# Split weights at staggered places in SBUF and right-hand pools 192 bytes lower, in a two-layer decoder trunk

## The chip, the cores and the metric

The kernel runs on one core of one Trainium2 chip. The metric is device time in microseconds (us) of one execution. In traces and groups the engines are PE (TensorE, matmul), PEld (its weight load), DVE (VectorE), ACT (ScalarE), POOL (GpSimd) and SP (SyncE, which issues most transfers).

## The reference

Two pre-norm residual layers and a final norm, on one sequence of 1024 tokens, width 1024, in float32. Layer 0 mixes with eight retention heads and eight RWKV-7 heads that share one input and one output projection; layer 1 with sliding-window attention of 16 heads over 4 key/value heads. Each layer ends with a SwiGLU FFN of inner width 2816. Cut to what matters:

```python
for layer in range(2):
    h = rms_norm(x, norm1_g[layer])
    x = x + (retention_rwkv_mixer(h, ...) if layer == 0 else swa(h, ...))
    h = rms_norm(x, norm2_g[layer])
    x = x + (silu(h @ w_gate[layer]) * (h @ w_up[layer])) @ w_down[layer]
return rms_norm(x, final_g)
```

Nearly all of the arithmetic is in the projections and the FFN: float32 products of weights with activations.

## The kernel before

**Split products.** A float32 product is made from two halves in the reduced float32 type of PE (`F32R`). Each operand is split into a high part (a cast on ACT) and a low part (the operand minus the high part, a subtract on POOL, or on DVE where `self.lo` says so). `gemm` (L339 on) and `prod` (L1166 on) then issue three matmuls for each 128 x 128 block of weights: high by high, high by low, low by high (L345 to L347, L1169 to L1171; L239 where the mixer's planner issues them). Each of them loads 128 columns of weights, the stationary operand, and streams 512 columns of activations, the moving operand.

**Stages.** Tokens are taken in two halves of 512. Layer 0's mixer runs first, its order set by a planner (`Plan`) that keeps a running estimate of PE's time and picks chains and projection jobs by it. Then come the out projection of the first and of the second half, the FFN of layer 0 (gate and up in an early and a late part, then down), the attention of layer 1, its FFN and the final norm. The gate, up and down products are made by a seven-product scheme for 2 x 2 blocks (`early`, `late`, `form0`, `form1`); the late part streams combinations of activations that lie in the tiles `cb`, the early part streams the tiles `n8` (shown as `n`).

**Weights.** A raw block of 1024 columns is loaded to one of two places `wr` (L298). `wsplit` (L321 on) makes one or two split blocks of it, each 2 x 512 columns of 4 bytes, high part then low part. `wtile` (L312 on) gives the place for a split block: four rotating places `w` of 4096 bytes each in the left pool `pp`; in the late FFN the two `wr` places too; in the attention stage two places `wx` in the right-hand pool `at`; in a part of the down projection places `wd1` only. `wkept` (L305 on) takes the same four places for split blocks that are read back from DRAM.

**Where tiles lie.** Pools are stacks of SBUF: left ones grow upward from the bottom, right-hand ones downward from the top. `pp` is the lowest left pool and stays open; a tile `pad` of 120 columns is at the top of the right-hand stack. So the size of the `w` places shifts all that is allocated after them on the left (such as `n8` in `pp` and the later left pools), and the size of `pad` shifts every right-hand pool (such as `cb`, `at`, and `nB`, which holds an `n8` of layer 1). In bytes of a partition, before: `wr` at 2176 and 6272, `w` at 10368, 14464, 18560 and 22656, `n8` in `pp` from 27264, `pad` at 228864. Modulo 512: `w` and `wr` 128, `n8` on the left and `ha` 128, `n8` in `nB` 0, `cb` 0, `wx` 256, `wd1` 128.

**What sets the order.** The instructions of each engine are put in order when the kernel is built, by a scheduler with its own estimate of times; it works with tags and the number of buffers of each, not with addresses. On the chip each engine takes its instructions in that order and waits on semaphores.

Of the kernel before, what the change touches and what calls it, by code (L numbers as in the profile page):

```python
# [10 lines left out]
F32 = mybir.dt.float32  # L11
F32R = mybir.dt.float32r
# [4 lines left out]
P = 128  # L17
T = 1024
HT = 512
# [2 lines left out]
FT = 22  # L22
DGROUPS = [[(0, 4), (4, 8)], [(0, 4), (4, 8), (8, 11)]]
NP = FT // 2
CW = math.exp(-0.5)
NCH = 8
RMS_EPS = 1e-6
# [77 lines left out]
class Plan:  # L105
# [3 lines left out]
    def __init__(self, K):  # L109
        self.K, self.now, self.ev, self.banks = K, 0.0, {}, []  # L110
        self.gens, self.jobs, self.cur, self.twice = [], deque(), None, ()
# [93 lines left out]
class Kern:  # L205
    def __init__(self, ctx, tc, A, out):
        self.ctx, self.tc, self.nc, self.A, self.out = ctx, tc, tc.nc, A, out
        nc = self.nc
        self.pp = ctx.enter_context(tc.tile_pool(name="pp", bufs=1, side="left"))
        self.dr = ctx.enter_context(tc.tile_pool(name="dr", bufs=2, space=bass.MemoryType.DRAM))  # L210
        self.n = 0
        pad = ctx.enter_context(tc.tile_pool(name="pad", bufs=1, side="right"))
        pt = pad.tile([P, 120], F32, tag="pad", name="pad")
        nc.gpsimd.memset(pt, 0.0)
        nc.scalar.activation(pt[:, :16], pt[:, :16], AF.Copy)
        self.pv = self.t(self.pp, [P, NPV], "pv")
        nc.scalar.dma_start(self.pv, A["pvec"])
        self.cst = {}
        for nm in ("ones", "eps"):
            self.cst[nm] = self.const(self.pp, nm)  # L220
        self.h, self.plan = [None, None], None
        self.wx = None
        self.w6, self.nw, self.owed, self.lo = False, 0, [], self.nc.gpsimd
        self.hid = [self.dram(f"hid{i}", [FT, P, HT]) for i in range(4)]
        self.hc = [self.dram(f"hc{L}", [NP, 4, P, 2, HT]) for L in range(2)]
        self.bd = self.dram("bd", [KT, P, HT])
        self.u0d = self.dram("u0", [NP, 2, P, HT])
        self.wsp = self.dr.tile([30, 2, P, 2, HT], F32, tag="wsp", name="wsp", bufs=1)
        self.cats = [self.dram(f"cat{hf}", [KT, P, HT]) for hf in range(2)]
# [73 lines left out]
    def wkept(self, kept):  # L303

        res = []  # L305
        for i in range(2):
            w = self.t(self.pp, [P, 2, HT], "w", 4, F32R)
            self.nc.sync.dma_start(w.bitcast(F32), kept[i])
            res += [(w[:, 0, k * P : k * P + P], w[:, 1, k * P : k * P + P]) for k in range(4)]
        return res  # L310

    def wtile(self):  # L312

        pool, tag, n, only = self.wx or (None, "", 0, False)
        if only:
            return self.t(pool, [P, 2, HT], tag, n, F32R)
        i = self.nw = (self.nw + 1) % (6 if self.w6 else 4 + n)
        if i >= 4 and n:
            return self.t(pool, [P, 2, HT], tag, n, F32R)
        return self.t(self.pp, [P, 2, HT], *(("w", 4) if i < 4 else ("wr", 2)), F32R)  # L320

    def wsplit(self, raw, width=1024, keep=None):
        nc = self.nc
# [321 lines left out]
    def pair(self, u, hf, p):  # L645
# [38 lines left out]
        pw = self.t(mp, [P, HT], "rt", 6)  # L684
        S.activation(pw, cs, AF.Exp, scale=-CW)
        S.activation(cs, cs, AF.Exp, scale=CW)
        S.activation(s, s, AF.Exp, scale=-CW)
        PC = self.t(mp, [P, NCH], "PC", 4)
# [520 lines left out]
    def uses(self, L, p, sp, x=None):  # L1209
# [8 lines left out]
        def up(nm, c):  # L1218
            o = x[nm] if x else sg[nm]
            V.tensor_tensor(out=o, in0=sg[nm], in1=c, op=ALU.mult)  # L1220
            d = self.hid[2 * L + int(nm[1]) - 1][2 * p + int(nm[0]) - 1]
            if x and p == NP - 1:
                self.owed.append((d, o))
# [26 lines left out]
    def late_splits(self, L, wp):  # L1250

        def load(p):
            raws = [[self.rawtile(wp) for _ in range(2)] for _ in range(2)]
            for j in range(2):
                for i, nm in enumerate(("gate", "up")):
                    self.nc.sync.dma_start(raws[i][j], self.A[f"w_{nm}{L}"][2 * p + j])
            return raws

        nxt = load(0)
        for p in range(NP):  # L1260
            ws = [self.wsums(r, wp[0]) for r in nxt]
            if p == 0:
                yield
            if p + 1 < NP:
                nxt = load(p + 1)
# [25 lines left out]
    def form_down(self, L, p, x, ts):  # L1291
# [3 lines left out]
        def put(i, o, a, b):  # L1295
# [3 lines left out]
            d = (self.hc[L][p, i - 1], t.bitcast(F32))  # L1299
            if p == NP - 2 and i > 2:  # L1300
                self.owed.append(d)
# [188 lines left out]
    def attn(self, hf, nr, ap, n8):  # L1490
# [6 lines left out]
        def proj(ti, out, **kw):  # L1497
            w = self.wload(self.A["w_qkv"][ti])
            ps = self.pst("f", [P, HT])
            self.gemm(ps, w, nT)  # L1500
            V.tensor_tensor(out=out, in0=ps, in1=r, op=ALU.mult)
            S.activation(out, out, AF.Identity, **kw)
# [19 lines left out]
        for i, vc in enumerate(vcs):  # L1522
            pt = self.pst("m", [P, 4, P])
# [6 lines left out]
        for g in range(4):  # L1530
            for i in (2 * g, 2 * g + 1):
                proj(i, qt[i], scale=0.125, bias=b8[:, i : i + 1])
            for b in range(4):
                ti, rg = g // 2, g % 2
                k0 = 1 if (hf == 0 and b == 0) else 0
                kw = slice(P * k0, 256)
                nk = 256 - P * k0
                s = self.t(ap, [P, 4, 256], "s", 3)
                for e in range(2):
                    ps = self.pst("rc"[e], [P, 2, 256])  # L1540
                    a = slice(64 * e, 64 * e + 64)
                    src = (kc if e == rg else ks)[ti]
                    for i in range(2):
                        nc.tensor.matmul(
                            ps[:, i, kw], qt[2 * g + i][a, P * b : P * b + P], src[a, P * b + P * k0 : P * b + 256],
                            start=True, stop=True,
                        )
                    V.tensor_tensor(
                        out=s.rearrange("p (i e) k -> p e i k", e=2)[:, e, :, kw], in0=ps[:, :, kw],
                        in1=amask[:, kw].rearrange("p (o t) -> p o t", o=1).to_broadcast([P, 2, nk]), op=ALU.add,  # L1550
                    )
                st4 = self.t(ap, [P, 4, 4], "st4", 4)
                m, den, es = st4[:, 0, :], st4[:, 1, :], st4[:, 2, :]
                V.tensor_reduce(out=m, in_=s[:, :, kw], axis=AX.X, op=ALU.max)
                sk = sink[:, 4 * g : 4 * g + 4]
                V.tensor_tensor(out=m, in0=m, in1=sk, op=ALU.max)
                V.tensor_tensor(out=es, in0=sk, in1=m, op=ALU.subtract)
                V.tensor_scalar(out=m, in0=m, scalar1=-1.0, scalar2=None, op0=ALU.mult)
                S.activation(es, es, AF.Exp)
                for h in range(4):  # L1560
                    S.activation(
                        s[:, h, kw], s[:, h, kw], AF.Exp, bias=m[:, h : h + 1], accum_out=den[:, h : h + 1]
                    )
                V.tensor_tensor(out=den, in0=den, in1=es, op=ALU.add)
                V.reciprocal(out=den, in_=den)
                for h in range(4):
                    V.tensor_scalar(
                        out=s[:, h, kw], in0=s[:, h, kw], scalar1=den[:, h : h + 1], scalar2=None, op0=ALU.mult
                    )
                pT = self.t(ap, [P, 2, 4, P], "pT", 3)  # L1570
                for kb in range(k0, 2):
                    pt = self.pst("m", [P, 4, P])
                    for h in range(4):
                        nc.tensor.transpose(pt[:, h, :], s[:, h, P * kb : P * kb + P], ident)
                    if kb == 0:
                        S.copy(pT[:, kb], pt)
                    else:
                        V.tensor_copy(pT[:, kb], pt)
                po = self.pst("y", [P, 2, P])
                for e in range(2):  # L1580
                    a = slice(64 * e, 64 * e + 64)
                    pv4 = pT.rearrange("p k (i e) t -> p k e i t", e=2)
                    for kb in range(k0, 2):
                        nc.tensor.matmul(
                            po[a], vt[:, b + kb, 64 * g : 64 * g + 64], pv4[:, kb, e],
                            start=kb == k0, stop=kb == 1,
                        )
                tk = slice(P * b, P * b + P)
                hi, lo_ = n8[g][:, :, tk], n8[4 + g][:, :, tk]
                S.copy(hi, po)  # L1590
                V.tensor_tensor(out=lo_, in0=po, in1=hi.bitcast(F32), op=ALU.subtract)
# [234 lines left out]
```

## Time and profile before

| | us |
|---|---|
| median of 3 runs | 2416.72 |
| the runs | 2416.71, 2416.72, 2421.27 |
| span of the profiled execution | 2420.2 |
| PE busy in it | 2338.5 |
| DVE busy | 1635.1 |
| POOL busy | 1204.0 |
| ACT busy | 1035.8 |

All numbers from the trace belong to the one profiled execution. A row of groups gives line, engine, operation, output and inputs by the program's names without their numbers, partitions by columns, count, then the busy time of all in us and the mean of one in ns, then the idle time of the engine just ahead of them and what ended it. The ends of matmuls are modelled and overlap with the next start; their starts are recorded, and the timeline gives them in us from the start of the span.

### The profile page before, as it was taken

To read this page: it belongs to the slowest core of one execution; us is meant where nothing else is said; L and a number is where in the kernel's file an instruction comes from. 1 tells how busy PE (TensorE), PEld (TensorE's weight loads), DVE (VectorE), ACT (ScalarE), POOL (GpSimd) and SP (SyncE) were. 2 spreads that over 40 slices of the span, in tenths; PEclk is the share of its full clock that TensorE was granted. 3 is DMA by queue.
4 is the path that set the end of the run, shared out by engine and by line. 5 is a ranking of instruction groups with operands and counts; after the bars stand their busy time and mean duration, and the time that the engine had idled before them with its cause. 6 is when DMAs were issued, how large, how long until landed. Compare 5 with 4: busy or idle time off the path is not lost. (4 is left out here: it accounts for less than half of the span.)

```text
span 2420.2 us, 35718 instructions
## 1 busy us (share of the span) xinstructions
PE 2338.5 (97%) x13098; PEld 1838.3 (76%) x13098; DVE 1635.1 (68%) x2478; ACT 1035.8 (43%) x1914; POOL 1204.0 (50%) x975
## 2 busy tenths in 40 slices
PE   8999899989999999999999999999999999999997
PEld 6676677777777888887778877677678788887885
DVE  5766764776556457887675459558628787888776
ACT  5354543223555433333333545456635333333336
POOL 6555431221442057776577632342231677777665
PEclk9999999899999999999999999999999999999999
DMA  7564453434344645653564322142236466546652
GB/s 257 188 213 176 158 161 116 146 117 121 130 171 153 217 152 207 211 202 134 186 258 148 128 73 64 53 133 70 93 121 214 158 217 214 211 179 246 237 204 108
DMA packets 167742, 395.93 MB, mean 164 GB/s; under 512 B 42896, under 2 KB 45584, under 8 KB 167568
## 3 DMA queue, kind: packets, MB, share of 16 engines
q1 hardware_dynamic: 164448, 388.15, 47.2%
q10 hardware_dynamic: 2832, 4.45, 0.6%
q8 instruction: 104, 1.70, 0.3%
q0 software_dynamic: 288, 1.05, 0.1%
q14 instruction: 70, 0.57, 0.1%
HBM read 271.29 MB, written 116.92 MB: 160 GB/s over the span
## 5 line engine op out<-in xcount | busy, mean ns | idle before, releaser
L331 POOL TENSOR_TENSOR w<-wr,w 128x512 fp32r<-128x512 f32 x196 | 264.6, 1355 | 450.3 <-ACT w L330 391.5
L239 PE MATMUL ps_f<-n,w 128*128 128x512 f32 x1440 | 386.6, 417 | 13.5 <-ACT w L330 5.7
L239 PEld LDWEIGHTS ps_f<-n,w 128*128 128x128 f32 x1440 | 270.5, 193 | 97.3 <-issue 23.0
L330 ACT CAST w<-wr 128x512 fp32r<-128x512 f32 x244 | 148.0, 612 | 185.5 <-PE ps_f L347 77.5
L331 POOL TENSOR_TENSOR w<-wq,w 128x512 fp32r<-128x512 f32 x92 | 131.5, 1440 | 33.4 <-ACT w L330 28.8
L345 PE MATMUL ps_f<-n,w 128*128 128x512 f32 x356 | 142.2, 399 | 3.5 <-ACT n L351 2.6
L346 PE MATMUL ps_f<-n,w 128*128 128x512 f32 x356 | 142.9, 401 | 0.0
L347 PE MATMUL ps_f<-n,w 128*128 128x512 f32 x356 | 141.7, 398 | 0.0
L1176 DVE TENSOR_TENSOR nq<-ps_m,u 128x512 f32<-128x512 f32 x88 | 58.7, 684 | 108.8 <-PE ps_m L1171 108.5
L1169 PE MATMUL ps_f<-n,w 128*128 128x512 f32 x322 | 127.2, 396 | 4.1 <-DVE h L1369 1.8
L1170 PE MATMUL ps_f<-n,w 128*128 128x512 f32 x322 | 126.4, 392 | 0.0
L1171 PE MATMUL ps_f<-n,w 128*128 128x512 f32 x322 | 125.8, 391 | 0.0
L353 POOL TENSOR_TENSOR n<-nq,n 128x512 fp32r<-128x512 f32 x64 | 106.1, 1670 | 10.9 <-ACT n L351 10.9
L1171 PE MATMUL ps_m<-n,w 128*128 128x512 f32 x282 | 110.3, 391 | 0.0
L1170 PE MATMUL ps_m<-n,w 128*128 128x512 f32 x282 | 110.3, 391 | 0.0
L1169 PE MATMUL ps_m<-n,w 128*128 128x512 f32 x282 | 109.8, 390 | 0.0
L331 POOL TENSOR_TENSOR wx<-wr,wx 128x512 fp32r<-128x512 f32 (+1 forms) x38 | 49.3, 1299 | 105.0 <-ACT wx L330 105.0
L1169 PE MATMUL ps_m<-cb,w 128*128 128x512 f32 x240 | 94.8, 395 | 0.8 <-ACT w L330 0.8
L1171 PE MATMUL ps_m<-cb,w 128*128 128x512 f32 x240 | 94.8, 395 | 0.0
L1170 PE MATMUL ps_m<-cb,w 128*128 128x512 f32 x240 | 94.7, 395 | 0.0
L1343 POOL TENSOR_TENSOR w<-wd,w 128x512 fp32r<-128x512 f32 (+1 forms) x53 | 77.1, 1465 | 33.3 <-ACT w L1342 33.3
L345 PEld LDWEIGHTS ps_f<-n,w 128*128 128x128 f32 x356 | 67.4, 189 | 21.7 <-ACT n L351 3.0
(525 smaller groups left out, 6495.5 us busy)
## 6 DMA issues: line engine op xcount, KB each, us to landing
hc<-n SPq DMA_DIRECT2D x74, 512.0 KB, 2.7
wsp<-w SPq DMA_DIRECT2D x54, 512.0 KB, 3.4
w<-wsp SPq DMA_DIRECT2D x54, 512.0 KB, 3.6
wq<-in_w_gate SPq DMA_DIRECT2D x44, 512.0 KB, 3.9
u<-u SPq DMA_DIRECT2D x88, 256.0 KB, 2.9
n<-hc SPq DMA_DIRECT2D x43, 512.0 KB, 5.2
wr<-in_w_in SPq DMA_DIRECT2D x34, 512.0 KB, 4.8
hid<-n SPq DMA_DIRECT2D x66, 256.0 KB, 2.0
```

The source lines that it names most:

```text
L239: self.nc.tensor.matmul(out, lhsT, rhs, **kw)
L330: nc.scalar.copy(hi[:, :n], raw[:, c])
L331: self.lo.tensor_tensor(out=lo[:, :n], in0=raw[:, c], in1=hi.bitcast(F32)[:, :n], op=ALU.subtract)
L345: nc.tensor.matmul(ps, hi, rh, start=k == 0, stop=False)
L346: nc.tensor.matmul(ps, hi, rl, start=False, stop=False)
L347: nc.tensor.matmul(ps, lo, rh, start=False, stop=k == n - 1)
L353: e.tensor_tensor(out=lo, in0=src, in1=hi.bitcast(F32), op=ALU.subtract)
L1169: mm(ps, hi, xh, start=first and k == 0, stop=False, skip_group_check=True)
L1170: mm(ps, hi, xl, start=False, stop=False, skip_group_check=True)
L1171: mm(ps, lo, xh, start=False, stop=last and k == len(w) - 1, skip_group_check=True)
L1176: add = lambda o, x, y: V.tensor_tensor(out=o, in0=x, in1=y, op=ALU.add)
L1343: nc.gpsimd.tensor_tensor(out=lo, in0=v, in1=hi.bitcast(F32), op=ALU.subtract)
```

## The change

The four places for split weights, one tag with four buffers before, become four tags `w0` to `w3` with one buffer each, taken in turn by a new function `wplace`. Each place is longer by an unused piece: 16, 16, 8 and 8 columns of 4 bytes, that is 64, 64, 32 and 32 bytes. `pad` grows from 120 to 168 columns, 192 bytes. The small tile `st4` of the attention, four buffers of 64 bytes, becomes four of 128, of which the first 64 are used; this lowers what is allocated below it in `at` (such as `wx`) by 256 bytes more.

```diff
+WPAD = (16, 16, 8, 8)
...
-        pt = pad.tile([P, 120], F32, tag="pad", name="pad")
+        pt = pad.tile([P, 168], F32, tag="pad", name="pad")
...
+        self.iw = 3
...
-            w = self.t(self.pp, [P, 2, HT], "w", 4, F32R)
+            w = self.wplace()
...
-        return self.t(self.pp, [P, 2, HT], *(("w", 4) if i < 4 else ("wr", 2)), F32R)
+        return self.wplace() if i < 4 else self.t(self.pp, [P, 2, HT], "wr", 2, F32R)
+
+    def wplace(self):
+
+        self.n, self.iw = self.n + 1, (self.iw + 1) % 4
+        w = self.pp.tile([P, 2 * HT + WPAD[self.iw]], F32R, tag=f"w{self.iw}", name=f"w{self.iw}_{self.n}", bufs=1)
+        return w[:, : 2 * HT].rearrange("p (a b) -> p a b", b=HT)
...
-                st4 = self.t(ap, [P, 4, 4], "st4", 4)
+                st4 = self.t(ap, [P, 32], "st4", 4)[:, :16].rearrange("p (a b) -> p a b", b=4)
```

After: `wr` at 2176 and 6272 as before, `w0` to `w3` at 10368, 14528, 18688 and 22816, `n8` in `pp` from 27456, `pad` at 228672. Modulo 512: `wr` and `w0` 128, `w1` 192, `w2` 256, `w3` 288, every moving tile of a split product 320, `wx` and `wd1` 320.

Every engine but DVE has as many rows in its order as before (PE 8885, POOL 971); no instruction is added or removed. The scheduler moves a few blocks against each other. In the rows below, a name is followed by the numbers of its tiles, and lines of the changed kernel are larger by 8.

On PE, in the out projection of the second half of layer 0, two column blocks of weights follow each other, `ps_f_7034` and `ps_f_7068`. Before:

```order
L345 MATMUL ps_f_7034<-n_1002_6799,w_7031 128x512
L346 MATMUL ps_f_7034<-n_1006_6803,w_7031 128x512
L347 MATMUL ps_f_7034<-n_1002_6799,w_7031 128x512
L345 MATMUL ps_f_7034<-n_1002_6799,w_7031 128x512
L346 MATMUL ps_f_7034<-n_1006_6803,w_7031 128x512
L347 MATMUL ps_f_7034<-n_1002_6799,w_7031 128x512
```

After:

```order
L354 MATMUL ps_f_7034<-n_1006_6803,w_1057_7031 128x512
L353 MATMUL ps_f_7068<-n_1000_6797,w_1060_7062 128x512
L354 MATMUL ps_f_7068<-n_1004_6801,w_1060_7062 128x512
L355 MATMUL ps_f_7068<-n_1000_6797,w_1060_7062 128x512
L353 MATMUL ps_f_7068<-n_1000_6797,w_1060_7062 128x512
L354 MATMUL ps_f_7068<-n_1004_6801,w_1060_7062 128x512
L355 MATMUL ps_f_7068<-n_1000_6797,w_1060_7062 128x512
L353 MATMUL ps_f_7068<-n_1001_6798,w_1060_7062 128x512
L354 MATMUL ps_f_7068<-n_1005_6802,w_1060_7062 128x512
L355 MATMUL ps_f_7068<-n_1001_6798,w_1060_7062 128x512
L353 MATMUL ps_f_7068<-n_1001_6798,w_1060_7062 128x512
L355 MATMUL ps_f_7034<-n_1002_6799,w_1057_7031 128x512
```

Ten matmuls of the second block (`ps_f_7068`) have moved into the first one, behind its first two with `w_7031`.

On POOL, the subtracts that make the low parts of the weights for the same blocks. Before:

```order
L331 TENSOR_TENSOR w_6945<-wr_6940,w_6945 128x512
L331 TENSOR_TENSOR w_7028<-wr_7026,w_7028 128x512
L331 TENSOR_TENSOR w_7031<-wr_7026,w_7031 128x512
L331 TENSOR_TENSOR w_7062<-wr_7060,w_7062 128x512
L331 TENSOR_TENSOR w_7065<-wr_7060,w_7065 128x512
L331 TENSOR_TENSOR w_7096<-wr_7094,w_7096 128x512
```

After:

```order
L339 TENSOR_TENSOR w_1051_6945<-wr_6940,w_1051_6945 128x512
L339 TENSOR_TENSOR w_1060_7062<-wr_7060,w_1060_7062 128x512
L339 TENSOR_TENSOR w_1056_7028<-wr_7026,w_1056_7028 128x512
L339 TENSOR_TENSOR w_1057_7031<-wr_7026,w_1057_7031 128x512
L339 TENSOR_TENSOR w_1061_7065<-wr_7060,w_1061_7065 128x512
L339 TENSOR_TENSOR w_1064_7096<-wr_7094,w_1064_7096 128x512
```

The subtract for `w_7062`, the first weights of the second block, has moved ahead of both subtracts of the first block. On ACT the cast that belongs to it moves likewise. A second place is in the early FFN of layer 1, where ten matmuls of `ps_f_2515` stand behind 24 of the `ps_m` that follows it. The four places are taken in turn, as before.

## Prediction

> **What bounds the kernel now.** I read the page's busy times first, then the table of stages, then the groups of instructions with their shapes, then PE's timeline.
>
> ```profile
> span 2420.2 us, 35718 instructions
> PE 2338.5 (97%) x13098; PEld 1838.3 (76%) x13098; DVE 1635.1 (68%) x2478; ACT 1035.8 (43%) x1914; POOL 1204.0 (50%) x975
> 770.00:880.00 110.00, 110.00 (x487) 91.09 (x486) 59.29 (x88) 46.82 (x84) 17.21 (x13) 1.00 0.60 206
> 880.00:1160.00 280.00, 279.15 (x1211) 226.83 (x1210) 214.70 (x234) 96.22 (x163) 192.01 (x133) 1.00 0.53 183
> 1890.00:2190.00 300.00, 297.58 (x1288) 241.23 (x1287) 243.88 (x260) 106.44 (x182) 212.42 (x149) 1.00 0.56 200
> ```
>
> In a row of stages stand its length, then the busy time of PE, of its weight load, of DVE, ACT and POOL, then the granted clock. PE is the bound: 97% of the span, and in the three stages shown (early FFN of layer 0, then the late FFN of both layers) it never rests and has its full clock. There a nanosecond more or less in each matmul is a nanosecond of the span. The profiled execution's span, 2420.2 us, stands 3.5 us above the median of the runs, 2416.72; I work out differences and put them on the median.
>
> The change leaves every matmul in place and alters only where its two operands lie. So the question is whether the time of a matmul depends on that. Before, it does by name of tile:
>
> ```profile
> L1169 PE MATMUL ps_m<-cb,w 128*128 128x512 f32 x240 | 94.8, 395 | 0.8 <-ACT w L330 0.8
> L1171 PE MATMUL ps_m<-cb,wr 128*128 128x512 f32 x112 | 44.2, 395 | 0.0
> L1169 PE MATMUL ps_c<-n,w 128*128 128x512 f32 x80 | 31.1, 389 | 0.0
> L1169 PE MATMUL ps_c<-n,wr 128*128 128x512 f32 x37 | 14.4, 389 | 0.0
> L345 PE MATMUL ps_f<-ha,wd 128*128 128x512 f32 x48 | 18.7, 389 | 0.0
> ```
>
> The same shape takes 395 ns with cb streaming, 389 ns with n or ha, whichever tile the weights are in. Matmuls overlap, so what counts is the step from start to start, which PE's timeline gives (start, modelled length, operation), first in the early FFN, then in the late one:
>
> ```profile
> 800.30 0.39 PE L1171 MATMUL ps_f<-n,w 128*128 128x512 f32 x1
> ...
> 803.02 0.39 PE L1171 MATMUL ps_f<-n,w 128*128 128x512 f32 x1
> ```
> ```profile
> 881.01 0.40 PE L1170 MATMUL ps_m<-cb,w 128*128 128x512 f32 x1
> ...
> 882.19 0.39 PE L1169 MATMUL ps_m<-cb,w 128*128 128x512 f32 x1
> 882.41 0.40 PE L1170 MATMUL ps_m<-cb,w 128*128 128x512 f32 x1
> ...
> 884.28 0.40 PE L1169 MATMUL ps_m<-cb,w 128*128 128x512 f32 x1
> ```
>
> From 800.30 to 803.02 lie 12 steps: 2.72 us, 226.7 ns each. From 881.01 to 884.28 lie 14: 3.27 us, 233.6 ns each.
>
> Where the operands lie, the built program says. In a partition, modulo 512 bytes, the weights w and wr begin at 128 and wx at 256; ha tiles and most n tiles begin at 128, but cb tiles and those n tiles that sit in the right-hand pool of layer 1 at 0. So the rows at 389 have a difference of 0 and those at 395 one of 128. That it is the address, and not cb or its stage, the attention stage of layer 1 shows:
>
> ```profile
> 1553.65 0.39 PE L345 MATMUL ps_f<-n,w 128*128 128x512 f32 x1
> ...
> 1556.20 0.40 PE L347 MATMUL ps_f<-n,w 128*128 128x512 f32 x1
> 1556.43 0.39 PE L345 MATMUL ps_f<-n,wx 128*128 128x512 f32 x1
> ...
> 1561.64 0.40 PE L347 MATMUL ps_f<-n,wx 128*128 128x512 f32 x1
> ```
> ```profile
> 1590.37 0.40 PE L345 MATMUL ps_f<-n,wx 128*128 128x512 f32 x1
> ...
> 1595.73 0.40 PE L347 MATMUL ps_f<-n,wx 128*128 128x512 f32 x1
> ```
>
> In the first, n lies at 0. With w (difference 128), 11 steps from 1553.65 to 1556.20 take 2.55 us, 232 ns each; with wx (difference 256), 23 steps from 1556.43 to 1561.64 take 5.21 us, 226.5 ns each, for the same n tiles. In the second, n lies at 128 and wx is the one that costs (difference 128): 23 steps, 5.36 us, 233 ns each. So 0 and 256 are clean and 128 costs 5.5 to 7 ns, whatever the tile. I use 6 (395 less 389).
>
> **The change, part by part.** Counted in the built programs, 8,364 matmuls have 512 columns and split operands. Before, 5,580 of them have a difference of 0, 2,532 one of 128 (1,584 of these stream cb), and 252 one of 256. After, all moving tiles begin at 320 and the weights at 128, 192, 256 and 288 in turn (places 0 to 3), so the weights lie below the moving tile by 192 in 3,030 matmuls (place 0 and the two raw places), by 128 in 1,578 (place 1), by 64 in 1,593 (place 2), by 32 in 1,575 (place 3), and by 0 in 588 (wx and the wd1 places).
>
> *Removed:* what the 2,532 lose now: 2,532 x 6 ns = 15.2 us.
>
> *Added, 128 below:* 1,578 x 6 ns = 9.5 us. All cases of the trace have the weights 128 above. As 0 and 256 are alike, the pattern seems to repeat every 256, and then 128 below is 128 above. If it does not, nothing: the ends are 0 and 9.5, and I take 9.5.
>
> *Added, 192, 64 and 32 below:* 3,030 + 1,593 + 1,575 = 6,198 matmuls at differences that no row shows. The nearest rows are the clean one and the one at 128, so the ends are 0 and 6,198 x 6 ns = 37.2 us. No step under 226 ns is to be seen in the clean stretch, but between the cb rows single steps are shorter (882.19 to 882.41), so an end below 0 stays open; it is priced with the rivals. I take 0: 192 is 64 above if the pattern repeats, so all three lie within 64 of a clean difference and at least 64 from the bad one. That is a choice between far ends, and the chances below treat it so.
>
> *Sum of these:* -15.2 + 9.5 + 0 = -5.7 us. The sum changes sign where the 6,198 lose 5.7 us / 6,198 = 0.92 ns each.
>
> *The order.* The new tags move a few blocks. The place where PE waits is layer 0's out projection of the second half (PE, POOL and ACT on the timeline):
>
> ```profile
> 717.85 0.47 PE L345 MATMUL ps_f<-n,w 128*128 128x512 f32 x1 [2.57 <-ACT n L351]
> 718.16 0.45 PE L346 MATMUL ps_f<-n,w 128*128 128x512 f32 x1
> ```
> ```profile
> 718.36 1.29 POOL L331 TENSOR_TENSOR w<-wr,w 128x512 fp32r<-128x512 f32 x1 [1.80 <-ACT w L330]
> ```
> ```profile
> 717.14 0.62 ACT L351 CAST n<-u 128x512 fp32r<-128x512 f32 x1 [3.81 <-DVE u L1117]
> 717.66 0.61 ACT L330 CAST w<-wr 128x512 fp32r<-128x512 f32 x1
> ```
>
> Ten matmuls of the next column block now stand inside the first one, and POOL subtracts that block's first weights ahead of the first block's. A cast (0.62 us) and a subtract (1.29 us) may come ahead of what PE needs: between 0 and 1.9 us, or a little below 0 if the ten fill a wait. The 2.57 us end on the cast of n, whose place has not moved, so I take 0. In layer 1's early FFN ten matmuls move behind 24 that are as ready, in a stage without idle time: 0.
>
> *The other engines.* They read the same moved tiles:
>
> ```profile
> L331 POOL TENSOR_TENSOR w<-wr,w 128x512 fp32r<-128x512 f32 x190 | 259.8, 1373 | 436.6 <-ACT w L330 377.8 <-DVE sg L1220 52.8 <-DMA wr<-in_w_in 2.4
> L330 ACT CAST w<-wr 128x512 fp32r<-128x512 f32 x238 | 145.8, 617 | 185.3 <-PE ps_f L347 77.5 <-PE ps_f L239 26.5 <-PE ps_m L1171 25.0
> L239 PE MATMUL ps_f<-n,w 128*128 128x512 f32 x1440 | 386.6, 417 | 13.5 <-ACT w L330 5.7 <-POOL w L331 4.0 <-DVE n L462 3.8
> ```
>
> POOL is busy half the span and waits 436.6 us ahead of this group alone, so a subtract that grew or shrank by some per cent stays under PE's 97%; PE itself waits only 4.0 us for it in the largest group. If that cover were gone, 5% on 259.8 us would be 13 us. I cost it at 0. The larger pad adds 48 columns to one memset at the start, before any matmul: 0. No place is added or taken away and the ring stays at four, so no wait is new.
>
> *Sum:* -5.7 + 0 (order) + 0 (other engines) = -5.7 us: 2416.7 - 5.7 = **2411.0 us**. Its own ends are -15.2 (128 below is clean too: 2401.5) and -5.7 + 1.9 = -3.8 (2412.9).
>
> A rule that speaks against any effect: the Trainium skill, page "SBUF — State Buffer", section "Who interferes with whom", gives PE two independent read ports, one for the moving operand and one for the weight load, and says that PE never waits on anyone; by it the sum would be 0. The trace disagrees: 226.5 ns against 232 and 233 for one shape, by address alone.
>
> **The rivals.**
>
> *Slower: the clean setting is narrow.* The weight load (76% busy, under the running matmul) would lose against the moving stream at every difference that is no multiple of 256. The change takes 7,776 matmuls off the clean setting and puts in order only 2,532. With half the price (3 ns) at 192, 64 and 32 the sum is 6,198 x 0.003 + 9.5 - 15.2 = +12.9 us, 2429.6; with the whole price 37.2 + 9.5 - 15.2 = +31.5 us, 2448.2. It decides from a mean of 0.92 ns over the 6,198 on, and it would show first in stages that run clean now, such as 770 to 880 us. For it: the trace has two clean differences and both are the same one if the pattern repeats, so nothing says how wide the clean part is. Against it: only that none of the three is more than a quarter of the repeat away from a clean one.
>
> *Nothing: gain and loss cancel.* If one of the two larger classes, 192 or 64, costs about 3 ns and the other none, the sum is -5.7 + 9.1 = +3.4 or -5.7 + 4.8 = -0.9 us: 2420 or 2416. That PE's addresses do not matter at all would give 2416.7 as well, but the rows at 1556 us exclude it.
>
> *Faster than forecast: 226.7 ns holds a collision itself.* In the cb stream steps of 0.22 and 0.24 mix. If all 7,776 new matmuls took 0.225, 1.7 ns less, 13.2 us more would go than in the cleanest case: -15.2 - 13.2 = -28.4 us, 2388. The Trainium skill, page "TensorE: Matmul & The Clock Gate", section "Back-to-back issue gap", puts a 512-column matmul at about 216 ns in isolation; no run here shows that. Against it: no step in the clean stretches is that short.
>
> **How the numbers follow.** A measurement of this kernel tells about 0.2% (4.8 us) from no change, so faster is below 2411.9 and slower above 2421.6. Forecast: 0.36, of which 0.32 lies below 2411.9 and 0.04 above, for the order's price; faster than forecast: 0.10; cancelled: 0.14; slower at about half the price: 0.28; slower at the whole price: 0.12. That makes 0.42 for faster (0.32 + 0.10), 0.18 for the same (0.04 + 0.14) and 0.40 for slower (0.28 + 0.12). The range runs from 2392, which leaves out some 0.07 of the 0.10 below, to 2440, which leaves out the 0.12 at the whole price. The forecast's own range is 2401.5 to 2412.9.
>
> **What would show it.** Right: cb with w falls from 395 to a mix of 389 and, in one place of four, 395; n with w rises to 395 in that place alone; the steps of a stretch by place of weights read 226.7, 233, 226.7, 226.7; the means of casts, subtracts and sums on the other engines stay. Wrong: steps above 226.7 ns in most places between 770 and 880 us (the slower rival), or below 226 anywhere for long (the faster one). A mean above 0.92 ns over 226.7 in places 0, 2, 3 and the raw places makes the sign wrong, whatever the rest does.

## The result, and the profile after

| | us |
|---|---|
| before, median of 4 runs | 2418.99 |
| after, median of 4 runs | 2442.16 (2439.56 to 2446.01) |
| ratio | 1.0093 (95% interval 1.0076 to 1.0110) |
| span of the profiled execution after | 2441.6 |

The changed kernel takes 0.93% longer, some 22.5 us. The forecast was 2411.0 us, its range 2392 to 2440.

The page after, span and busy times:

```profile
span 2441.6 us, 35711 instructions
PE 2364.3 (97%) x13098; PEld 1839.6 (75%) x13098; DVE 1641.6 (67%) x2478; ACT 1037.7 (43%) x1914; POOL 1209.3 (50%) x975
```

The span grew by 21.4 us and PE's busy time by 25.8 (2338.5 before). DVE, ACT and POOL stand where they stood, to 0.5%: the other engines did not feel the addresses. The groups that were 395 and 389 before, now (lines larger by 8):

```profile
L1177 PE MATMUL ps_m<-cb,w 128*128 128x512 f32 x240 | 94.7, 395 | 0.6 <-DVE nq L1184 0.6
L1177 PE MATMUL ps_c<-n,w 128*128 128x512 f32 x80 | 31.6, 395 | 0.0
L1177 PE MATMUL ps_c<-n,wr 128*128 128x512 f32 x37 | 14.6, 394 | 0.0
L353 PE MATMUL ps_f<-ha,wd 128*128 128x512 f32 x48 | 18.7, 389 | 0.0
```

cb with w has not become cheaper, n with w and with wr has risen from 389 to 395 and 394, and only ha with wd, whose difference is 0 as before, is still at 389. The stretch of the early FFN that took 226.7 ns a step before, on PE's timeline after:

```profile
800.05 0.40 PE L1178 MATMUL ps_f<-n,w 128*128 128x512 f32 x1
...
803.32 0.40 PE L1178 MATMUL ps_m<-n,w 128*128 128x512 f32 x1
```

From 800.05 to 803.32 lie 14 steps: 3.27 us, 233.6 ns each.

For each class of address difference (beginning of the weights less beginning of the moving tile, modulo 512) I took all steps from start to start under 300 ns between two split matmuls in a row, in the whole trace, each put to the class of its first matmul. That is the list to which the experiments below add:

| difference | before, ns | after, ns |
|---|---|---|
| 0 | 227.6 | 228.4 |
| 256 | 228.8 | |
| +128 | 232.9 | |
| -128 | | 232.5 |
| -192 | | 233.1 |
| -64 | | 230.6 |
| -32 | | 233.3 |
| all | 229.32 | 232.25 |

2.93 ns more in each of 8,364 matmuls is 24.5 us, which is the whole of what the time lost, and slightly more.

### The profile page after: what moved, and what is told of

Same layout as the page of the kernel before. It is cut to its first block, busy times and chain, and to the rows that moved or that the text cites. A ratio compares the mean times of both kernels' runs of the same rounds, so it can differ in the third digit from the quotient of the medians.

```text
span 2441.6 us, 35711 instructions
## 1 busy us (share of the span) xinstructions
PE 2364.3 (97%) x13098; PEld 1839.6 (75%) x13098; DVE 1641.6 (67%) x2478; ACT 1037.7 (43%) x1914; POOL 1209.3 (50%) x975
## 4 chain that ended last, share of the span: by engine, by line
PE 73%; DVE 11%; ACT 5%; DMA 4%; issue 4%; POOL 2%; SPq 1%; DVEq 0%; ACTq 0%; POOLq 0%
PE ps_f L241 8%; PE ps_m L1177 7%; PE ps_m L1179 7%; PE ps_m L1178 7%; PE ps_m L241 5%; PE ps_f L353 5%; PE ps_f L354 5%; PE ps_f L355 5%; PE ps_f L1179 3%; PE ps_f L1178 3%; PE ps_f L1177 3%; PE ps_r L1177 2%; PE ps_r L1179 2%; PE ps_r L1178 2%; PE ps_c L1179 2%
## 5 line engine op out<-in xcount | busy, mean ns | idle before, releaser
L241 PE MATMUL ps_f<-n,w 128*128 128x512 f32 x1440 | 391.3, 420 | 12.7 <-ACT w L338 6.2
L353 PE MATMUL ps_f<-n,w 128*128 128x512 f32 x356 | 144.8, 407 | 2.6 <-ACT n L359 1.6
L355 PE MATMUL ps_f<-n,w 128*128 128x512 f32 x356 | 144.0, 405 | 1.4 <-POOL w L339 1.4
L354 PE MATMUL ps_f<-n,w 128*128 128x512 f32 x356 | 145.2, 408 | 0.0
L1177 PE MATMUL ps_f<-n,w 128*128 128x512 f32 x322 | 128.4, 400 | 2.2 <-ACT w L338 1.0
L1178 PE MATMUL ps_f<-n,w 128*128 128x512 f32 x322 | 127.3, 395 | 0.0
L1179 PE MATMUL ps_f<-n,w 128*128 128x512 f32 x322 | 127.0, 395 | 0.0
L353 PEld LDWEIGHTS ps_f<-n,w 128*128 128x128 f32 x356 | 68.3, 192 | 21.6 <-issue 2.5
```

The costliest lines, as they stand in the source:

```text
L241: self.nc.tensor.matmul(out, lhsT, rhs, **kw)
L353: nc.tensor.matmul(ps, hi, rh, start=k == 0, stop=False)
L354: nc.tensor.matmul(ps, hi, rl, start=False, stop=False)
L355: nc.tensor.matmul(ps, lo, rh, start=False, stop=k == n - 1)
L1177: mm(ps, hi, xh, start=first and k == 0, stop=False, skip_group_check=True)
L1178: mm(ps, hi, xl, start=False, stop=False, skip_group_check=True)
```

## The experiments

The theory after the result (A): each address difference has a price of its own per matmul, and only few differences are clean. Rivals: (B) it is the changing of the difference from place to place that costs; (C) it is the new order of the instructions; (D) it is the other engines. All ratios are to the kernel before, run beside it.

### One difference everywhere, in the order of before

`u0`: only the pad is longer, so that every split matmul has a difference of 0 or 256.

```diff
-        pt = pad.tile([P, 120], F32, tag="pad", name="pad")
+        pt = pad.tile([P, 216], F32, tag="pad", name="pad")
```

> The kernel before with its pad 384 bytes longer and nothing else: all 8,364 split matmuls then have an address difference of 0 or 256, and the order of PE, ACT, DVE and SP is that of before. Theory A (each difference has its own price per matmul; in the two traces the mean step is 227.6 ns at 0, 232.9 at 128): 2,532 matmuls lose 5.3 ns less each, -13.4 us, ratio 0.9945, and all cb groups fall from 395 to 389 or 390 ns. Rival (the change was slow for its order or for the other engines, addresses being a small matter): within 0.2% of before.

Measured: 2412.73 us, ratio 0.9966 (0.9950 to 0.9981). The groups, and a stretch of cb on the timeline:

```profile
L1169 PE MATMUL ps_m<-cb,w 128*128 128x512 f32 x240 | 93.5, 389 | 0.9 <-DVE nq L1176 0.9
L1169 PE MATMUL ps_c<-n,w 128*128 128x512 f32 x80 | 31.1, 389 | 0.0
```
```profile
883.82 0.39 PE L1171 MATMUL ps_m<-cb,w 128*128 128x512 f32 x1
...
886.99 0.39 PE L1171 MATMUL ps_m<-cb,wr 128*128 128x512 f32 x1
```

cb, the same tile in the same stage, now takes 14 steps in 3.17 us, 226.4 ns each, and 389 in its group. So the price of cb was its address. Steps at 0 have a mean of 227.5 ns. The gain is 8.2 us (4.6 to 12.1) where 13.4 were expected.

`um32`, `um64`, `um192`, `up64`: a gap of S bytes between the weights and the left moving tiles, and the pad longer by R bytes, so that 7,776 matmuls have one difference. S and R are 32 and 352, 64 and 320, 192 and 192, 448 and -64; for `um32`:

```diff
-        pt = pad.tile([P, 120], F32, tag="pad", name="pad")
+        pt = pad.tile([P, 208], F32, tag="pad", name="pad")
...
+        self.gap = []
...
     def n8(self, pool):

+        if not self.gap:
+            self.gap = [self.pp.tile([P, 8], F32, tag="gap", name="gap", bufs=1)]
+            self.nc.gpsimd.memset(self.gap[0], 0.0)
```

> The kernel before with all weights of 7,776 matmuls 32 bytes below the moving tile modulo 512, the same difference everywhere. Theory A (own price, 233.2 ns at -32 in the trace after): 7,776 x 5.6 ns = 43.5 us over the clean kernel, +30 us against before, ratio 1.0125. Theory B (the price after comes from changing the difference with every place of weights, not from the difference): about the clean kernel, 0.9945.

> All weights of 7,776 matmuls 64 bytes below. Theory A (230.3 to 230.6 ns at -64 in the trace after): 7,776 x 2.8 ns = 22 us over the clean kernel, +8 us against before, ratio 1.0035; if what follows the other places in the trace after made these steps longer, less. Theory B (changing differences cost): about 0.9945.

> All weights of 7,776 matmuls 192 bytes below. Theory A (233.2 ns at -192 in the trace after): 7,776 x 5.6 = 43.5 us over the clean kernel, +30 us against before, ratio 1.0125. Theory B (changing differences cost): about 0.9945. If -192 is like +64 and the price depends only on the distance from a multiple of 256, this run should equal the one at -64.

> All 7,776 matmuls with the weights 64 bytes above the moving tile, in the order of before. If the pattern repeats every 256 bytes, it is the same as -192: 233.3 ns per step, ratio 1.0075. If it repeats only every 512, something else; if it is symmetric, as -64: 229.6 ns, ratio 1.000.

| run | difference | step, ns | us | ratio |
|---|---|---|---|---|
| um32 | -32 | 233.3 | 2437.93 | 1.0076 (1.0058 to 1.0094) |
| um64 | -64 | 229.6 | 2421.13 | 0.9999 (0.9986 to 1.0013) |
| um192 | -192 | 233.4 | 2438.29 | 1.0073 (1.0057 to 1.0090) |
| up64 | +64 | 233.3 | 2440.73 | 1.0084 (1.0062 to 1.0107) |

The same stretch of the early FFN in the run at -32, then in the one at -64:

```profile
799.65 0.39 PE L1174 MATMUL ps_m<-n,w 128*128 128x512 f32 x1
...
802.45 0.39 PE L1174 MATMUL ps_f<-n,w 128*128 128x512 f32 x1
```
```profile
799.71 0.39 PE L1174 MATMUL ps_f<-n,w 128*128 128x512 f32 x1
...
802.46 0.39 PE L1173 MATMUL ps_m<-n,w 128*128 128x512 f32 x1
```

Twelve steps each: 2.80 us (233.3 ns) and 2.75 us (229.2 ns). At -32 and -192 the steps with one difference everywhere are those of the same class in the trace after, to 0.3 ns; at -64 they are 1.0 ns shorter. So B falls as the cause: the difference itself has the price, and it is nearly the whole one even 32 bytes from a clean one. Up to 1 ns at -64 may still come from changing differences. -192 and +64 agree to 0.1 ns a step, so the pattern does repeat every 256 bytes, as the prediction took it; but -64 and +64 differ by 3.7 ns, so it is not the distance from a clean difference that counts. Three of the four times stay below what A's sum gave (1.0125 at -32 and -192, 1.0035 at -64); only +64 is above the 1.0075 that was expected from the run at -192. Where the rest goes is taken up below.

### The order alone, and a mixture in the old order

`a0`: the changed kernel with its four tags, and so its order, but all differences 0.

```diff
-WPAD = (16, 16, 8, 8)
+WPAD = (0, 0, 0, 0)
...
-        pt = pad.tile([P, 168], F32, tag="pad", name="pad")
+        pt = pad.tile([P, 216], F32, tag="pad", name="pad")
```

> The changed kernel with its four tags and therefore its order of instructions, but no bytes between the places and the pad 384 bytes longer than before: every one of the 8,364 split matmuls has a difference of 0. If the order costs nothing (the term of 0 in the prediction), it equals the clean kernel in the order of before: ratio 0.9966 to the kernel before. If the order costs what the jump at the out projection and the stall ahead of it suggest in the trace after (about 2 to 8 us): 0.9975 to 1.000, and a wait of PE for POOL of about 1.4 us at the place that the prediction showed.

Measured: 2411.61 us, ratio 0.9963 (0.9950 to 0.9976), within 0.03% of the kernel with the old order. C falls: over the whole kernel the order costs nothing that these runs can tell, and they tell some 5 us, so it can't have made the 22.5. It does cost at the place that the prediction showed, the out projection of the second half; PE's timeline in the trace after, and in `a0`:

```profile
723.30 0.47 PE L353 MATMUL ps_f<-n,w 128*128 128x512 f32 x1 [1.59 <-ACT n L359]
...
725.44 0.80 PE L355 MATMUL ps_f<-n,w 128*128 128x512 f32 x1 [1.43 <-POOL w L339]
```
```profile
715.19 0.47 PE L353 MATMUL ps_f<-n,w 128*128 128x512 f32 x1 [1.78 <-ACT n L359]
...
717.32 0.79 PE L355 MATMUL ps_f<-n,w 128*128 128x512 f32 x1 [1.43 <-POOL w L339]
```

PE waits less for n (1.59 and 1.78 us against 2.57) and then 1.43 us for POOL's low part, which now comes behind another block's subtract: 1.59 + 1.43 - 2.57 = 0.45 us more in the one, 1.78 + 1.43 - 2.57 = 0.64 in the other. The two waits are not all of it. From the first matmul of the out projections to the first of the FFN, `a0` takes 73.6 us and `u0`, clean too but in the old order, 69.3. Of these 4.3 us some 2.6 lie in 13 steps of about 427 ns, at a granted clock of 0.50; `u0` has none there, the kernel before has 8, and `scan2` and `scan3` below, in the new order, have none. So in these executions the order adds some 0.5 us of waits there; whether it brings the steps at half clock too is not shown.

`mix64`: four places under one tag as before, each 64 bytes longer, moving tiles at 384, so that 3,015 matmuls have -256, 1,593 -192, 1,575 -128 and 1,593 -64.

```diff
+    def wplace(self):
+
+        return self.t(self.pp, [P, 2 * HT + 16], "w", 4, F32R)[:, : 2 * HT].rearrange("p (a b) -> p a b", b=HT)
...
-        pt = pad.tile([P, 120], F32, tag="pad", name="pad")
+        pt = pad.tile([P, 152], F32, tag="pad", name="pad")
```

> Four places 64 bytes further apart each, under one tag as before, so in the order of before; the moving tiles at 384: differences -256 (3,015 matmuls of the first place and the raw ones, beside 444 of wx), -192 (1,593), -128 (1,575) and -64 (1,593). Theory A (own prices over the clean 227.5: 5.8 at -192, 5.3 at -128, 2.1 at -64, and -256 as 0): 9.2 + 8.3 + 3.3 = 20.8 us over the clean kernel in this order, that is about 2412.7 + 20.8 = 2433.5, ratio 1.005. Theory B (changing the difference costs by itself, about 0.8 ns more per matmul as -64 shows in the trace after): 6 us more, 1.008. The steps by place decide between them.

Measured: 2420.41 us, ratio 1.0004 (0.9986 to 1.0021). The steps by place are as theory A has them: 228.1 at -256, 233.2 at -192, 232.7 at -128, 230.0 at -64. The time is not: 20.8 us over `u0` were expected, and the two ratios are 9.2 us apart (1.0004 less 0.9966). So the prices of the steps hold, but their sum is more than the time shows.

Where the rest goes, the pages of the runs say in part: the span less PE's busy time is 81.7 us before and 68.3 at -32 (2434.0 less 2365.7).

```profile
span 2434.0 us, 35719 instructions
PE 2365.7 (97%) x13098; PEld 1837.7 (76%) x13098; DVE 1639.9 (67%) x2478; ACT 1036.4 (43%) x1914; POOL 1210.0 (50%) x976
```

In the run at -32, PE waits 13 us less. In the mixer of layer 0 (the first 650 us, 1,473 split matmuls) the steps at -32 are 4.05 ns longer than before, 6.0 us in all, and the stage is 1.4 us longer; its idle time falls from 37.2 to 30.2 us. There PE waits for chains on the other engines, and a longer step may only shorten the wait. The runs don't show that it always does. At +64 the step and the order are those of -192, but the same stage takes 650.8 us against 644.9, and PE's idle time in it is 38.0 us against 30.0; the other stages agree to 3 us. So this stage differs by some 6 us from one profiled execution to another for reasons other than the steps.

### How wide the good differences are

`scan1`, `scan2` and `scan3` give the four places of the changed kernel other differences; in the last two the block sits some bytes into its place.

```diff
-WPAD = (16, 16, 8, 8)
+WPAD = (16, 16, 16, 16)
+WOFF = (4, 4, 12, 4)
...
-        return w[:, : 2 * HT].rearrange("p (a b) -> p a b", b=HT)
+        return w[:, WOFF[self.iw] : WOFF[self.iw] + 2 * HT].rearrange("p (a b) -> p a b", b=HT)
```

This is `scan2`, with a pad of 152 columns and `st4` as before the change; `scan3` has WOFF = (2, 12, 14, 12); `scan1` has WPAD = (16, 16, 16, 8), no WOFF and a pad of 160, both with `st4` as in `scan2`.

> The changed kernel with the places at four other differences, -224 (3,030 matmuls), -160 (1,578), -96 (1,593) and -32 (1,575), moving tiles at 352. It measures three prices not yet seen. If the price depends on the distance from a multiple of 256 alone, -224 costs what -32 costs (233.3 ns) and -160 what -96 costs. If it depends on the difference modulo 64, all four cost about what -32 costs. -32 itself should read 233.3 again.

> The changed kernel with places 64 bytes longer each, the block inside its place moved by 16, 16, 48 and 16 bytes, moving tiles at 384: differences -240 (1,605 matmuls, 16 above a clean one), -176 (1,578), -80 (1,593) and -48 (1,575), beside 1,425 raw ones at -256. It asks how wide the two good differences, 0 and -64, are. If addresses count in units of 32 bytes, -240 costs what -256 does (228 ns) and -48 what -64 does (230), -176 and -80 about 233. If the good differences are single points, all four cost about 233. If the price rises with distance, -240 lies at 229 to 231.

> As the run before it, with the block moved by 8, 48, 56 and 48 bytes: differences -248 (1,605 matmuls, 8 above a clean one), -144 (1,578), -72 (1,593, 8 below -64) and -16 (1,575, 16 below a clean one). Units of 32 bytes counted from the place: -248 costs 228, -72 and -144 and -16 about 233. A price that rises with distance: -248 and -72 near 229 and 231, -16 between 229 and 231. Single points: all about 233.

Mean steps by difference, of these and of the runs above:

| difference | step, ns | | difference | step, ns |
|---|---|---|---|---|
| 0 | 227.5 | | -96 | 233.0 |
| -16 | 228.6 | | -128 | 232.5 to 232.7 |
| -32 | 233.3 | | -144 | 233.1 |
| -48 | 232.0 | | -160 | 233.9 |
| -64 | 229.6 | | -176 | 231.8 |
| -72 | 231.9 | | -192 | 233.4 |
| -80 | 230.5 | | -224, -240, -248 | 233.1, 233.0, 231.0 |

None of the three expected shapes holds. Clean are 0 (or 256) and nearly -16; -64 and -80 cost 2 to 3 ns; all else costs 3.5 to 6.4. It is no function of the distance, and it is finer than 32 bytes. What the memory does to make it so stays open.

The times are 2440.92 (1.0086, 1.0054 to 1.0119), 2426.92 (1.0031, 1.0014 to 1.0048) and 2412.11 (0.9967, 0.9952 to 0.9983). The last did not fit A: its steps have a mean of 230.28 ns, those of `u0` 227.53, and the two take the same time. Its profile has another difference, in POOL's subtracts:

```profile
L340 POOL TENSOR_TENSOR w<-wr,w 128x512 fp32r<-128x512 f32 x190 | 243.7, 1287 | 441.9 <-ACT w L339 438.0 <-DVE z L632 1.8 <-issue 1.4
```

1373 ns on average before, 1287 here: where the block lies 8 or 56 bytes into its place, the median subtract into it takes 1093 and 1097 ns, at 48 bytes 1292 and 1298. That called for a test of D by itself.

### POOL's subtracts by themselves

`raw8`: raw weights (in `wr` and in the raw tiles of the late FFN) lie 8 bytes into their places, so that source and result of a subtract are 8 bytes apart modulo 16. That reaches 362 of POOL's 504 operations of 128 x 512 on weight tiles; the others stay at multiples of 16, but for two. As many matmuls as before, 2,532, lie 128 apart modulo 256. `best2`: the same with a pad of 152 columns, which puts all of them at 0 or 256.

```diff
-        raw = self.t(self.pp, [P, 1024], "wr", 2)
+        raw = self.wrt(2)
...
+    def wrt(self, o, dt=F32):
+
+        return self.t(self.pp, [P, 1088], "wr", 2, dt)[:, o : o + 1024]
...
-        return self.t(wp[i // 4], [P, 1024], f"wq{i}", 1) if i < 6 else wp[2][i - 6]
+        return self.t(wp[i // 4], [P, 1040], f"wq{i}", 1)[:, 2 : 1024 + 2] if i < 6 else wp[2][i - 6]
```

> The kernel before with raw weights 8 bytes into their places (wr when it holds raw weights, longer by 256 bytes, and the raw tiles of the late FFN), so that the source and the result of POOL's subtract lie 8 bytes apart modulo 16; the split matmuls keep their differences, 2,532 of them at 128 modulo 256. In the run with blocks moved by 8 and 56 bytes, such a subtract took 1092 ns instead of 1292, undisturbed, and the time equalled the clean kernel's although its steps were 2.8 ns longer. If POOL's subtracts sat on the path, the groups of w from wr and wq fall to about 1150 and 1250 ns and the time by some 10 us, ratio 0.996. If the time of that run had another cause, the groups fall and the time stays, ratio 1.000.

> The same with the pad 128 bytes longer, so that every split matmul has a difference of 0 or 256. If both effects are real and add up: 0.9966 x 0.996 = 0.993. If PE's steps alone matter: as the clean kernel, 0.9966.

Measured: `raw8` 2405.28 us, ratio 0.9938 (0.9922 to 0.9955); `best2` 2392.83 us, ratio 0.9890 (0.9872 to 0.9909). The subtract from wq in the kernel before (that from wr is in the prediction), the two in `raw8`, and the page of `best2`:

```profile
L331 POOL TENSOR_TENSOR w<-wq,w 128x512 fp32r<-128x512 f32 x92 | 131.5, 1440 | 33.4 <-ACT w L330 28.8 <-DVE nq L1176 4.6
```
```profile
L337 POOL TENSOR_TENSOR w<-wr,w 128x512 fp32r<-128x512 f32 x190 | 222.7, 1176 | 456.5 <-ACT w L336 398.1 <-DVE sg L1226 52.9 <-issue 2.7
L337 POOL TENSOR_TENSOR w<-wq,w 128x512 fp32r<-128x512 f32 x92 | 113.6, 1243 | 45.4 <-ACT w L336 40.7 <-DVE nq L1182 4.7
```
```profile
span 2391.4 us, 35718 instructions
PE 2319.0 (97%) x13098; PEld 1834.2 (77%) x13098; DVE 1601.3 (67%) x2478; ACT 1037.7 (43%) x1914; POOL 1133.9 (47%) x975
```

From 1373 and 1440 the subtracts fall to 1176 and 1243, and 15 us (11 to 19) leave the time although POOL is busy only half of it. The profiled executions are 16.3 us apart. The mixer of layer 0 is 11.1 us shorter (644.3 to 633.2 us for the same matmuls), of which some 2.6 are fewer steps at half clock, and the attention and the early FFN of layer 1 are 6.0 and 1.9 us shorter; the rest is 2.7 longer. In the attention all of it lies in steps into or out of matmuls that are not split (136.7 to 130.7 us). DVE is relieved too, 1635.1 to 1596.4 us in `raw8`, also in rows that read no raw weights: `n<-nq,nq` falls from 1391 to 1266 ns (1328 in `u0`). Whether the 15 us come through POOL's own shorter subtracts or through DVE's shorter operations, these runs don't separate. The two effects, of clean differences and of moved raw weights, add: 0.9966 x 0.9938 = 0.9904, measured 0.9890. `best2` beats both kernels of this study.

D is true of another change, not of this one: in the changed kernel the blocks moved by multiples of 32 bytes and POOL's times stayed (1209.3 us busy against 1204.0).

## Why the prediction was wrong

**What bounds the kernel: right.** PE's step was the quantity that moved, and 24.5 us of longer steps stand against 22.5 us in the time.

**That the address sets the step: right.** `u0` shows it on cb itself. The Trainium skill, page "SBUF — State Buffer", section "Who interferes with whom", calls PE's read ports for the moving operand and for the weight load independent. If that is taken to mean that their addresses don't matter, as the rival rule in the prediction took it, the traces disagree by up to 6.4 ns in 227.5; that another engine's reads slow a matmul here, no run shows. One reading was wrong: the single step of 0.22 us in the cb stream (882.19 to 882.41) is the rounding of the printed starts. In the trace's nanoseconds that step is 229, and the steps of the stretch alternate between 229 and 237 or 238. So the stretch gave no sign of steps shorter than the clean ones.

**Removed, 15.2 us at 6 ns:** in the step list 5.4 ns, 2,532 x 5.4 = 13.7 us. Of this `u0` gets 8.2.

**128 below, 9.5 us:** right in kind, 232.5 less 227.5 is 5.0 ns, 7.9 us. That the pattern repeats every 256 is confirmed by -192 and +64.

**192, 64 and 32 below, 0: this is the step that failed.** The prediction took the value of the clean end because the three lie within 64 bytes of a clean difference. They cost 5.6, 3.1 and 5.8 ns in the trace after: 3,030 x 5.6 = 17.0, 1,593 x 3.1 = 4.9 and 1,575 x 5.8 = 9.1, in all 31.0 us of the 37.2 that were its upper end. Distance from a clean difference was no measure of the price: -32 is the nearest of the three and the dearest. Put into the sum, -13.7 + 7.9 + 31.0 = +25.2 us; the time shows +22.5.

**The order, 0:** not told from 0 over the whole (`a0`, to some 5 us). At the place named the waits grow by 0.45 to 0.64 us, inside the bounds of 0 to 1.9; with the steps at half clock around it the two out projections of `a0` take 4.3 us more than those of `u0`, which is outside, but such steps come in the old order too.

**The other engines, 0:** right for this change. But the reason given, that POOL's idle time covers a subtract that changes, did not hold: `raw8` shortens the subtracts by 197 ns and gains 15 us, through POOL or through DVE.

**The rivals:** the one that ended slower, that the clean setting is narrow, is what happened, between its half price (2429.6) and its whole price (2448.2). It had a chance of 0.40 in all, and the range ended at 2440, 2 us under the result, because only 0.12 was given to the whole price. The trace of before had no row at a fourth of the repeat, and for an unknown of that size the two ends deserved about the same weight.

What stays open is why the sum of longer steps reaches the time to nine tenths in the change and to six tenths in the uniform runs at -32 and -192 (26.6 and 25.9 us over `u0` where 45 are in the steps). Shorter waits in the mixer take up part of it at -32 and -192, but not at +64, where 28.6 us came. Another part may be the clock: in the trace after, 60 split matmuls of the mixer stepped at about 427 ns, at a granted clock of 0.50, against 42 before and 42 at -32, and 18 x 0.2 us is 3.6 us. The intervals of these ratios, about 5 us wide to each side, leave room for the rest.

## What to carry to other kernels

Where PE never rests, look at the steps from start to start of equal matmuls and sort them by the address difference of weights and moving tile before touching anything else: the clean kernel here needed one pad. Do not interpolate between known differences; measure each, which one run can do for four of them by giving rotating places one difference each. And the idle time of an engine that feeds PE is no proof that its operations are covered: try a shorter one.

## What the runs showed of the hardware that was not expected

The mean step of a split 512-column matmul depends on the address difference modulo 256, between 227.5 and 233.9 ns, with a fine structure below 32 bytes. The median subtract of 128 x 512 on POOL takes 1292 to 1301 ns when its operands lie a multiple of 16 bytes apart and 1093 to 1097 when they lie 8 apart modulo 16 (`scan3`, `raw8`); ACT's casts do not change (617 ns before, 618 in `scan3` and `raw8`).

Single steps of 306 ns appear in the late FFN of `u0`, about every 27.4 us, some of them in pairs. Two of them on its timeline:

```profile
1031.68 0.47 PE L1169 MATMUL ps_m<-n,wr 128*128 128x512 f32 x1
1031.99 0.40 PE L1170 MATMUL ps_m<-n,wr 128*128 128x512 f32 x1
```
```profile
1059.09 0.47 PE L1169 MATMUL ps_m<-n,w 128*128 128x512 f32 x1
1059.39 0.39 PE L1170 MATMUL ps_m<-n,w 128*128 128x512 f32 x1
```

They cost about 1 us in each late FFN stage. `a0` has them too, and the run at -64 every 27.6 us, which is about 120 of its steps as in `u0`; the kernel before has none in these stages, and neither has `best2`, though all its differences are clean. Their cause was not tried.
